# Row blocks of three, the last columns in halves and the last store in three pieces, in a windowed matrix product on one Trainium2 core

## The chip, the cores and the metric

The kernel runs on 1 core of one Trainium2 chip. The metric is the device time of one execution in microseconds (us). All timed runs compared here are of the fast state (two slow executions of the kernel before, 210.19 and 194.12 us, are left out); the five probe runs are single runs, whose state is unknown and whose time is not used.

## The reference

```python
B, S, D, W = 4, 4096, 4096, 64          # x is [B, S, D], w is [D, D], both fp32
for b in range(B):
    o = int(offsets[b])
    results.append(x[b, o:o+W] @ w)      # four windows of 64 rows, one matrix
return np.stack(results).astype(np.float32)
```

The 4 x 64 window rows are two groups `g` of 128. The matrix has 67 MB and is read once; that is most of the traffic of 75.5 MB.

## The kernel before

The matrix comes in by row blocks of 128 rows each ("row" in this text often means such a row of blocks, `ki` from 0 to 31). Up to row 21 whole rows are loaded, several in one DMA; from row 22 on (`k_tail`) the two column halves are loaded and finished one after the other, half 1 first. All these loads but that of row 0 are issued by GpSimd and are cast to fp16 on the way; row 0 comes by SP and ACT as fp32 and is cast by ACT.

```python
blocks = [(0, 1), (1, 1), (2, 4), (6, 4), (10, 4), (14, 4), (18, 2), (20, 2)]
k_tail = 22
...
order = [1, 0]
for ng in order:
    big = wc_pool.tile([P, R_MAX * N], fp16, name="wc", tag="wc")
    small = w1_pool.tile([P, N], fp16, name="w1", tag="w1")
    ki = k_tail
    while ki < n_k:
        n = 1 if ng == order[-1] and ki >= n_k - 2 else 2
        ...                                       # one DMA for n rows of this half
...
q = [nc.scalar, nc.sync]
for ng in order:
    ...
    for ki in kts:
        for g in range(G):
            for j in range(n_sub):                # 4 column tiles of 512
                ...
                mm(4 * g + j, g, ki, rhs, ki == kts[0], ki == kts[-1])
    for g in range(G):
        for j in range(n_sub):
            add_out(4 * g + j, g, ng * n_sub + j) # VectorE: acc += PSUM bank
    for g in range(G):
        (nc.gpsimd if ng == order[0] else q[g]).dma_start(
            out=out[2 * g : 2 * g + 2, :, ng * NG : (ng + 1) * NG],
            in_=acc[g][:, ng * NG : (ng + 1) * NG],
        )
```

## Time and profile before

| | before |
|---|---|
| median of 3 runs | 182.32 us (182.32 to 182.44) |
| profiled span | 180.37 us |
| HBM read and written | 71.30 + 4.19 MB, 419 GB/s |
| last stores issued (ACT, SP) | 172.83 and 175.21 us |

The way to read it is shown in the prediction below. In short: the DMA engines are full from start to end, TensorE waits for them in places, and the end is four stores of 1 MB, two of which fill the DMA engines while the other two are still being computed.

### The profile page before, as it was taken

The page shows a single profiled execution, that of the slowest core. Times are in us where ns is not written, and L with a number is a line of the kernel's source. Part 1 is how long each engine was busy: PE and PEld are TensorE (multiplying, and loading weights), DVE is VectorE, ACT ScalarE, POOL GpSimd, SP SyncE. Part 2 cuts the span into 40 slices and gives each one's busy share as a digit, 9 for nine tenths or more (in the row PEclk, how much of TensorE's full clock was granted, in tenths as well). Part 3 has the DMA queues.
Part 4 walks back from the last instruction along what each step waited for, and adds up shares of the span by engine and source line. Part 5 has one row for each costly group of instructions (what it writes and reads, how often), then busy time and mean ns, then how long its engine had stood idle before and what let it go on. Part 6 is the DMA issues. An engine that isn't in the chain of part 4 may idle for free.

```text
span 180.4 us, 1501 instructions
## 1 busy us (share of the span) xinstructions
PE 127.1 (70%) x576; PEld 57.8 (32%) x576; DVE 79.2 (44%) x120; ACT 14.4 (8%) x19; POOL 15.2 (8%) x30
## 2 busy tenths in 40 slices
PE   0000789504999399908996599999789998898900
PEld 0000774101344144303442244444234443343400
DVE  0000667400587277811886167899920007300280
ACT  2422546400000000000000000000000000000000
POOL 4600000000000100020002400041011001100000
PEclk9999999965799999996999879999999999999975
DMA  5999989999998899999999999999999999999986
GB/s 185 314 254 216 273 189 196 236 233 225 233 233 174 182 233 233 238 218 233 196 196 203 225 207 207 225 193 214 215 213 216 213 214 214 216 212 214 362 367 265
DMA packets 4936, 40.98 MB, mean 227 GB/s; under 512 B 450, under 2 KB 450, under 8 KB 3010
## 3 DMA queue, kind: packets, MB, share of 16 engines
q0 software_dynamic: 4352, 36.70, 94.2%
q1 hardware_dynamic: 288, 2.10, 3.1%
q10 hardware_dynamic: 290, 2.10, 2.8%
q8 instruction: 4, 0.07, 0.1%
q14 instruction: 2, 0.02, 0.0%
HBM read 71.30 MB, written 4.19 MB: 419 GB/s over the span
## 4 chain that ended last, share of the span: by engine, by line
DMA 57%; PE 29%; another core or an unknown queue 5%; issue 3%; DVE 1%; POOLq 1%; POOL 1%; DVEq 1%
DMA wc<-in_w_dram 57%; PE bank L143 29%; DVE acc L153 1%; POOLq L68 1%; DVEq L227 1%; POOL xrow L75 0%; POOL identity masks.py:197 0%; POOLq L75 0%; DVEq L153 0%; POOL w L64 0%; POOLq masks.py:199 0%; POOLq L216 0%
## 5 line engine op out<-in xcount | busy, mean ns | idle before, releaser
L143 PE MATMUL bank<-wc,xT 128*128 128x512 f16 x448 | 106.0, 394 | 25.1 <-DMA wc<-in_w_dram 22.4
L153 DVE TENSOR_TENSOR acc<-acc,bank 128x512 f32<-128x512 f32 x104 | 68.1, 685 | 72.8 <-PE bank L143 72.2
L143 PEld LDWEIGHTS <-xT 128*128 128x128 f16 x512 | 51.2, 101 | 93.6 <-DMA wc<-in_w_dram 23.6
L129 PE MATMUL bank<-identity,xrow 128*128 128x128 f16 x64 | 7.1, 312 | 19.6 <-DMA xrow<-in_x_dram 19.6
L138 DVE CAST xT<-bank 128x512 f16<-128x512 f32 x8 | 5.5, 692 | 21.5 <-PE bank L129 21.5
L143 PE MATMUL bank<-w,xT 128*128 128x512 f16 x64 | 14.6, 385 | 0.0
L129 PEld LDWEIGHTS <-xrow 128*128 128x128 f16 x64 | 6.7, 148 | 19.8 <-issue 19.8
L108 POOL DMA_DIRECT2D wc<-in_w_dram x8 | 5.6, 710 | 42.4 <-PE bank L143 36.0
L92 POOL DMA_DIRECT2D wc<-in_w_dram x6 | 3.2, 545 | 67.7 <-PE bank L143 67.7
L168 DVE COPY acc<-bank 128x512 f32<-128x512 f32 x8 | 5.5, 692 | 1.6 <-PE bank L143 1.4
L140 ACT CAST xT<-bank 128x512 f16<-128x512 f32 x8 | 4.7, 585 | 8.2 <-PE bank L129 8.2
L170 ACT COPY acc<-bank 128x512 f32<-128x512 f32 x8 | 4.7, 585 | 2.5 <-PE bank L143 2.5
L198 POOL DMA_DIRECT2D out_dram<-acc x2 | 1.1, 536 | 18.5 <-DVE acc L153 18.5
L108 POOL DMA_DIRECT2D w<-in_w_dram x3 | 1.8, 607 | 8.6 <-DMA wc<-in_w_dram 8.6
L61 ACT CAST w<-acc 128x2048 f16<-128x2048 f32 x1 | 1.9, 1897 | 4.7 <-DMA acc<-in_w_dram 4.7
L75 POOL DMA_DIRECT2D xrow<-in_x_dram x4 | 2.1, 524 | 2.1 <-issue 2.1
L60 ACT CAST w<-acc 128x2048 f16<-128x2048 f32 x1 | 1.9, 1897 | 2.9 <-DMA acc<-in_w_dram 2.9
L60 ACT ACT_TABLE_LOAD x1 | 1.3, 1283 | 1.8 <-PEq L216 1.8
L64 POOL DMA_DIRECT2D w<-in_w_dram x1 | 0.7, 667 | 0.8 <-POOLq L216 0.8
masks.py:199 POOL TENSOR_SCALAR_AFFINE_SELECT identity<-identity 128x128 f16<-128x128 f16 x1 | 0.3, 287 | 0.1
masks.py:197 POOL MEMSET identity<- 128x128 f16 x1 | 0.2, 223 | 0.0
L216 POOL MEMSET const-float32-0.0<- 128x1 f32 x1 | 0.1, 99 | 0.4 <-issue 0.4
(3 smaller groups left out, 0.3 us busy)
## 6 DMA issues: line engine op xcount, KB each, us to landing
wc<-in_w_dram POOLq DMA_DIRECT2D x4, 4096.0 KB, 48.3
wc<-in_w_dram POOLq DMA_DIRECT2D x8, 1024.0 KB, 36.5
wc<-in_w_dram POOLq DMA_DIRECT2D x2, 2048.0 KB, 38.8
w<-in_w_dram POOLq DMA_DIRECT2D x2, 1024.0 KB, 28.2
xrow<-in_x_dram POOLq DMA_DIRECT2D x4, 512.0 KB, 14.5
out_dram<-acc POOLq DMA_DIRECT2D x2, 1024.0 KB, 19.3
acc<-in_w_dram SPq DMA_DIRECT2D x1, 1024.0 KB, 5.1
acc<-in_w_dram ACTq DMA_DIRECT2D x1, 1024.0 KB, 11.2
```

The costliest lines, as they stand in the source:

```text
L60: nc.scalar.copy(out=w_one[0][:, :NG], in_=w0_32[:, :NG])
L61: nc.scalar.copy(out=w_one[0][:, NG:], in_=w0_32[:, NG:])
L75: nc.gpsimd.dma_start(out=x16[g][m * WIN : (m + 1) * WIN, :], in_=x[b][bass.ds(o, WIN), :],)
L92: nc.gpsimd.dma_start(out=t[:, base : base + r * N], in_=w[k0 * P : (k0 + r) * P, :].rearrange("(p r) n -> p (r n)", r=r),)
L108: nc.gpsimd.dma_start(out=t[:, c : c + n * NG].rearrange("p (t n) -> p t n", t=n), in_=w[ki * P : (ki + n) * P, ng * NG : (ng + 1) * NG].r ...
L129: nc.tensor.matmul(out=ps[t][:, i * P : (i + 1) * P], lhsT=x_cols(g, 4 * t + i), rhs=identity[:], start=True, stop=True,)
L138: nc.vector.tensor_copy(out=dst, in_=ps[t][:])
L140: nc.scalar.copy(out=dst, in_=ps[t][:])
L143: nc.tensor.matmul(out=ps[bank][:], lhsT=xT[g][:, kt * P : (kt + 1) * P], rhs=rhs, start=start, stop=stop,)
L153: nc.vector.tensor_add(out=dst, in0=dst, in1=ps[bank][:])
L168: nc.vector.tensor_copy(out=acc[g][:, c * NT : (c + 1) * NT], in_=ps[bank][:])
L170: nc.scalar.copy(out=acc[g][:, c * NT : (c + 1) * NT], in_=ps[bank][:])
```

## The change

The intent is a shorter end. Two rows of the matrix go from the column stage into blocks of three (fewer small packets). The last two rows of the last column half come in two quarters, so that half of the additions and stores can start earlier. ACT helps to empty the banks between the halves. The very last store is cut in pieces of 112, 8 and 8 rows, so that DMA engines 0 to 7 take nine rows and 8 to 15 take seven, on the premise that 8 to 15 are behind by then.

```diff
-    blocks = [(0, 1), (1, 1), (2, 4), (6, 4), (10, 4), (14, 4), (18, 2), (20, 2)]
-    k_tail = 22
+    blocks = [(0, 1), (1, 1), (2, 4), (6, 4), (10, 4), (14, 4), (18, 3), (21, 3)]
+    k_tail = 24
+    n_fine = 2
...
+    fine_steps = steps[: -(n_fine // 2)]
+    fine_steps.append((n_k - n_fine, n_fine, 0, NG // 2))
+    fine_steps += [(ki, 1, NG // 2, NG) for ki in range(n_k - n_fine, n_k)]
...
+    def store(eng, g, c0, c1, cuts=(0, P)):
+        for a, e in zip(cuts, cuts[1:]):
+            eng.dma_start(out=out_rows[g * P + a : g * P + e, c0:c1], in_=acc[g][a:e, c0:c1])
...
+    for g in range(G):
+        for j in range(0, n_sub, 2):
+            add_out(4 * g + j, g, ng * n_sub + j)
+            nc.scalar.copy(out=tmp[2 * g + j // 2][:], in_=ps[4 * g + j + 1][:])
...
+    for h in range(2):
+        js = range(h * n_sub // 2, (h + 1) * n_sub // 2)
...
+            c0 = ng * NG + h * NG // 2
+            store(q[g], g, c0, c0 + NG // 2, (0, 112, 120, 128) if h == g == 1 else (0, P))
```

More of the change, by code (lines that the diff above doesn't have):

```diff
@@ L41 @@
     wc_pool = ctx.enter_context(tc.tile_pool(name="wc", bufs=3))
-    w1_pool = ctx.enter_context(tc.tile_pool(name="w1", bufs=2))
+    w1_pool = ctx.enter_context(tc.tile_pool(name="w1", bufs=1))
     acc_pool = ctx.enter_context(tc.tile_pool(name="acc", bufs=1))
@@ L49 @@
     xT = [x_pool.tile([P, D], fp16, name=f"xT{g}") for g in range(G)]
-    w_one = [w1_pool.tile([P, N], fp16, name="w1", tag="w1") for i in range(2)]
+    w_one = [w1_pool.tile([P, N], fp16, name=f"w1_{i}") for i in range(2)]
+    tmp = [acc_pool.tile([P, NT], fp32, name=f"tmp{i}") for i in range(4)]
     acc = [acc_pool.tile([P, N], fp32, name=f"acc{g}") for g in range(G)]
@@ L84 @@
     }
-    free = 0
     for k0, r in blocks[2:]:
-        if free < r:
-            t = wc_pool.tile([P, R_MAX * N], fp16, name="wc", tag="wc")
-            free = R_MAX
-        base = (R_MAX - free) * N
-        free -= r
+        t = wc_pool.tile([P, R_MAX * N], fp16, name="wc", tag="wc")
         nc.gpsimd.dma_start(
-            out=t[:, base : base + r * N],
+            out=t[:, : r * N],
             in_=w[k0 * P : (k0 + r) * P, :].rearrange("(p r) n -> p (r n)", r=r),
@@ L96 @@
         for q in range(r):
-            src[k0 + q] = lambda a, e, t=t, c=base + q * N: t[:, c + a : c + e]
+            src[k0 + q] = lambda a, e, t=t, c=q * N: t[:, c + a : c + e]
     tail = {}
     order = [1, 0]
-    for ng in order:
-        big = wc_pool.tile([P, R_MAX * N], fp16, name="wc", tag="wc")
-        small = w1_pool.tile([P, N], fp16, name="w1", tag="w1")
-        ki = k_tail
-        while ki < n_k:
-            n = 1 if ng == order[-1] and ki >= n_k - 2 else 2
-            n_in = (ki - k_tail) * NG
-            t, c = (big, n_in) if n_in < R_MAX * N else (small, n_in - R_MAX * N)
+    steps = [(ki, 2, 0, NG) for ki in range(k_tail, n_k, 2)]
+    fine_steps = steps[: -(n_fine // 2)]
+    fine_steps.append((n_k - n_fine, n_fine, 0, NG // 2))
+    fine_steps += [(ki, 1, NG // 2, NG) for ki in range(n_k - n_fine, n_k)]
+    for ng, st in zip(order, (steps, fine_steps)):
+        t = wc_pool.tile([P, R_MAX * N], fp16, name="wc", tag="wc")
+        pos = 0
+        for ki, n, c0, c1 in st:
+            wd = c1 - c0
             nc.gpsimd.dma_start(
-                out=t[:, c : c + n * NG].rearrange("p (t n) -> p t n", t=n),
-                in_=w[ki * P : (ki + n) * P, ng * NG : (ng + 1) * NG].rearrange(
+                out=t[:, pos : pos + n * wd].rearrange("p (t n) -> p t n", t=n),
+                in_=w[ki * P : (ki + n) * P, ng * NG + c0 : ng * NG + c1].rearrange(
                     "(t p) n -> p t n", p=P
@@ L114 @@
             for q in range(n):
-                tail[(ng, ki + q)] = t[:, c + q * NG : c + (q + 1) * NG]
-            ki += n
+                for j in range(wd // NT):
+                    a = pos + q * wd + j * NT
+                    tail[(ki + q, (ng * NG + c0) // NT + j)] = t[:, a : a + NT]
+            pos += n * wd
     def x_cols(g, kt):
@@ L177, with tail_mm @@
     whole_rows(last_block, range(order[1] * n_sub, (order[1] + 1) * n_sub), False)
-    q = [nc.scalar, nc.sync]
-    for ng in order:
-        kts = list(range(k_tail, n_k))
-        if ng == order[0]:
-            kts = list(last_block) + kts
-        for ki in kts:
-            for g in range(G):
-                for j in range(n_sub):
-                    c = ng * n_sub + j
-                    rhs = (
-                        src[ki](c * NT, (c + 1) * NT)
-                        if ki < k_tail
-                        else tail[(ng, ki)][:, j * NT : (j + 1) * NT]
-                    )
-                    mm(4 * g + j, g, ki, rhs, ki == kts[0], ki == kts[-1])
+    def tail_mm(ki, g, ng, j, start, stop):
+        c = ng * n_sub + j
+        rhs = src[ki](c * NT, (c + 1) * NT) if ki < k_tail else tail[(ki, c)]
+        mm(4 * g + j, g, ki, rhs, start, stop)
@@ L194 @@
+    out_rows = out.rearrange("b m n -> (b m) n")
+    def store(eng, g, c0, c1, cuts=(0, P)):
+        for a, e in zip(cuts, cuts[1:]):
+            eng.dma_start(out=out_rows[g * P + a : g * P + e, c0:c1], in_=acc[g][a:e, c0:c1])
+    ng = order[0]
+    kts = list(last_block) + list(range(k_tail, n_k))
+    for ki in kts:
         for g in range(G):
             for j in range(n_sub):
-                add_out(4 * g + j, g, ng * n_sub + j)
-        for g in range(G):
-            (nc.gpsimd if ng == order[0] else q[g]).dma_start(
-                out=out[2 * g : 2 * g + 2, :, ng * NG : (ng + 1) * NG],
-                in_=acc[g][:, ng * NG : (ng + 1) * NG],
-            )
+                tail_mm(ki, g, ng, j, ki == kts[0], ki == kts[-1])
@@ new lines @@
+    for g in range(G):
+        for j in range(0, n_sub, 2):
+            add_out(4 * g + j, g, ng * n_sub + j)
+            nc.scalar.copy(out=tmp[2 * g + j // 2][:], in_=ps[4 * g + j + 1][:])
+    for g in range(G):
+        for j in range(1, n_sub, 2):
+            c = ng * n_sub + j
+            dst = acc[g][:, c * NT : (c + 1) * NT]
+            nc.vector.tensor_add(out=dst, in0=dst, in1=tmp[2 * g + j // 2][:])
+        store(nc.gpsimd, g, ng * NG, (ng + 1) * NG)
+    ng = order[1]
+    k_fine = n_k - n_fine
@@ new lines @@
+    for ki in range(k_tail, k_fine):
+        for g in range(G):
+            for j in range(n_sub):
+                tail_mm(ki, g, ng, j, ki == k_tail, False)
+    q = [nc.scalar, nc.sync]
+    for h in range(2):
+        js = range(h * n_sub // 2, (h + 1) * n_sub // 2)
+        for ki in range(k_fine, n_k):
+            for g in range(G):
+                for j in js:
+                    tail_mm(ki, g, ng, j, False, ki == n_k - 1)
+        for g in range(G):
+            for j in js:
+                add_out(4 * g + j, g, ng * n_sub + j)
+            c0 = ng * NG + h * NG // 2
+            store(q[g], g, c0, c0 + NG // 2, (0, 112, 120, 128) if h == g == 1 else (0, P))
```

## The prediction

> **What bounds the kernel now.** I read the page first: its slices, queues and HBM line, and then the chain that ended last.
>
> ```profile
> PE   0000789504999399908996599999789998898900
> DMA  5999989999998899999999999999999999999986
> q0 software_dynamic: 4352, 36.70, 94.2%
> HBM read 71.30 MB, written 4.19 MB: 419 GB/s over the span
> DMA 57%; PE 29%; another core or an unknown queue 5%; issue 3%; DVE 1%; POOLq 1%; POOL 1%; DVEq 1%
> ```
>
> The reader is to see that the DMA row has 9 nearly everywhere while PE has holes, and that 71.30 + 4.19 = 75.49 MB in 180.4 us is 419 GB/s. (The GB/s row of the page shows half of that during loads, because it counts the fp16 that is written.) The matrix is read once, so no bytes can be saved; only time in which a DMA engine does nothing, or moves its bytes badly, can.
>
> So I asked for the mean DMA share by stage. Columns: stretch, length, busy us of PE, PEld, DVE, ACT, POOL, granted clock, DMA share, GB/s.
>
> ```profile
> 62.40:82.00 19.60, 14.02 (x65) 6.22 (x66) 11.00 (x16) 0.00 (x0) 1.05 (x2) 1.00 1.00 215
> 125.80:164.70 38.90, 35.47 (x152) 14.69 (x151) 11.17 (x19) 0.00 (x0) 2.84 (x5) 1.00 1.06 214
> 168.00:172.00 4.00, 3.79 (x18) 1.52 (x16) 1.69 (x3) 0.00 (x0) 0.00 (x0) 1.00 1.02 411
> 172.00:173.00 1.00, 0.00 (x0) 0.00 (x0) 1.00 (x3) 0.00 (x0) 0.00 (x0) 1.00 0.87 369
> 173.00:174.00 1.00, 0.00 (x0) 0.00 (x0) 1.00 (x3) 0.00 (x0) 0.00 (x0) 0.99 0.53 221
> 175.00:178.00 3.00, 0.00 (x0) 0.00 (x0) 0.18 (x1) 0.00 (x0) 0.00 (x0) 0.50 0.99 412
> 178.00:179.00 1.00, 0.00 (x0) 0.00 (x0) 0.00 (x0) 0.00 (x0) 0.00 (x0) 0.50 0.67 279
> ```
>
> The engines are full in the block stage and in the column stage alike. The only hole before the end is at 172 to 174 us: 0.13 + 0.47 = 0.6 us of the mean engine. Then the timeline of the end:
>
> ```profile
> 164.72 3.61 PE L143 MATMUL bank<-wc,xT 128*128 128x512 f16 x16 [0.73 <-DMA wc<-in_w_dram]
> 168.17 3.62 PE L143 MATMUL bank<-w,xT 128*128 128x512 f16 x16
> 170.31 4.87 DVE L153 TENSOR_TENSOR acc<-acc,bank 128x512 f32<-128x512 f32 x8 [15.39 <-PE bank L143]
> 172.83 0.35 ACTq L198 DMA_DIRECT2D out_dram<-acc  x1
> 175.21 0.35 SPq L198 DMA_DIRECT2D out_dram<-acc  x1
> ```
>
> It looks like a tail worth cutting: the last rows arrive, 16 matmuls and 8 additions follow, and two 1 MB stores end the kernel. But the other two 1 MB stores, those of the first column half, stand in the GpSimd queue behind all loads, and feed the DMA engines in just this time. That is why the hole is 0.6 us and not the 8 us from the last load to the last store.
>
> The last view is the trace's packet records (start, length, size, queue of each packet). Each transfer ends with one small completion packet per engine. Of the 16 for the last GpSimd store eleven are at 173.0 to 173.6 us and five at 174.1 to 174.6. Of the last store (SP) twelve lie at 179.1 to 179.2, the others up to 179.49. So five engines run up to 1.5 us late. In the load stream an engine drops back, and stays back, six times: after a 16 KB instruction fetch (four, at 34.8, 76.0, 115.9 and 145.8 us) by about 1.1 us, after an 8 KB one (two, at 73.3 and 130.4) by about 0.5. The late engines have no hole at 172 to 174: the first HWDGE store's packets interleave with what they still owe. **The slowest engine is busy without a break from start to 179.49 us, and it sets the end.** The eleven others idle about 1 us and reach the same end within 0.4 us.
>
> **What the Trainium skill says.** (1) "Perfetto Trace Analysis", section Roofline, says that a single active core is bounded by its 16 DMA engines, about 435 GB/s. The trace agrees: 419 over the whole span, and in the block stage 1.05 MB x 2 per row in 4.85 us, 433. (2) "DMA: Bandwidth & Descriptors", section Why small descriptors are slow, gives each packet about 3 cycles on top of one for each 32 bytes. With the 850 MHz of its bandwidth section, an 8 KB source packet is 259 cycles, 304.7 ns; the packet records show one start each 304.6 ns per engine. So I use it for the other sizes, as estimates. (3) The same page, section Why a DMA increments its semaphore by 16, says that a transfer uses the largest k up to 16 that divides its outer dimension, on SP and ACT the lowest k engines: 112 rows would be 7 for each of 16 engines, 8 rows one for each of engines 0 to 7. No record here names an engine; that the late ones are among 8 to 15 is the premise of the change, which I can't check. (4) Its section Issuing engines are not separate DMA queues says that all queues share the 16 engines, which the interleaving of three queues at 174 us shows.
>
> **The change, part by part.**
>
> Blocks of 3 and 3 in place of 2 and 2, column stage from row 24 instead of 22. Per engine and row: 2-row packets 8 x 1208 / 2 = 4.833 us, 3-row 8 x 1811 / 3 = 4.828, column packets 16 x 304.7 = 4.875. Before, 4 rows x 4.833 + 2 x 4.875 = 29.08; after, 6 x 4.828 = 28.97. It saves 0.11 us.
>
> The last two rows in halves. That is one row's worth of bytes in 4 KB pieces, estimated at 131 cycles or 154.1 ns each: 32 x 154.1 = 4.93 in place of 4.875, costs 0.06.
>
> The stores of the last half in quarters: 4 KB pieces again, 32 x 154.1 against 16 x 304.7, costs 0.06. Some more completion packets: 0.03. These parts together come to +0.03 us on every engine, so nothing.
>
> The 112, 8, 8 rows: engines 8 to 15 have 7 pieces instead of 8, one piece of 154 ns less; 0 to 7 have one more. If the late engines are all in 8 to 15 the end comes 0.15 us sooner.
>
> The tail off the DMA. The loads still end at about 169.6. PE: the chunk of rows 28 and 29 lands at 164.7, 16 matmuls to 168.4, then 8 for the first quarter pair (170.2), 8 for the second (172.0, 0.226 us each from the rows above). Additions at 4.87 / 8 = 0.61: 169.7 to 172.1 and 172.1 to 174.5. Stores issued at about 171.0, 172.2, 173.4 and 174.6 to 175.7 (three of 0.35 on SP). Before, they went out at 172.83 and 175.21. From issue to the first packet the ACT store took 1.2 us (174.05), so the first now reaches the engines near 172.2, before the GpSimd stores end: the hole of 0.6 us on the mean engine closes. But it is on the fast engines only, which then end at about 178.2 instead of 179.1. The slow one has no hole to close.
>
> The freed banks: four ACT copies (0.585 each from the ACT group of this shape) beside four additions free the banks in about 2.4 instead of 4.9 us between the column halves. PE needs it, since the change gives it more to do late: the second 3-row block lands near 130.4 us, after that 24 + 88 + 32 = 144 matmuls x 0.226 = 32.5 us and about 1 us for the eviction bring it to 163.9, just ahead of the landing at 164.7. So it is spent in slack too.
>
> Sum for the slowest engine: 179.49 + 0.03 - 0.15 = 179.37. Last completion to the end of the span was 180.37 - 179.49 = 0.88: span 180.25. Measured time minus span was 182.32 - 180.37 = 1.95: **182.2 us**. As the instruction fetches may fall a little better on a program with the work cut differently, I say 182.1.
>
> **Rivals.**
>
> (A) The tail counts in full. If the final 1 MB store, 16 matmuls and 8 additions really were the path, halving the last store (1.2 us) and half of the additions (2.4 us) would give about 179 us. For it stands the chain of waits, which ends in the additions. Against it, DMA share 0.99 from 175 to 178 and the late engines without a gap. I give it 5%.
>
> (B) PE becomes the bound. It idles about 2.6 us before the second 3-row block (block done near 127.8). After the idle of 3.80 us at 101.35 the clock was granted at half and matmuls took 0.43 us; after 3.06 at 62.42 it wasn't. If it falls here, PE loses about 1.6 us and the last stores are issued at 175.5 to 176.5. The engines have work until about 177, so up to 0.5 us would be lost: 182.2 to 182.8.
>
> (C) The fetches hit other engines, or one engine twice: a second lag of 1.1 us on one engine would give 183.3. If a fetch moved behind the end of the work or the late engines were spread better, 181.5. If the late engine is among 0 to 7, the extra row costs 0.15: 182.5.
>
> (D) Small stores to HBM interleaved from three queues are less efficient than estimated. In the last stores of before, packets took 305 to 335 ns where two queues met: 5% on 1 MB is 0.15 us.
>
> **Range and chances.** The sum gives 182.1; C and D spread it by about 0.5 on either side, B adds a little above. The range is 181.5 to 182.7. A gain of 2% would need 178.7, which only (A) gives; a loss of 2% would need 186.0, for which PE would have to fall far behind: faster 0.03, same 0.95, slower 0.02.
>
> **What would show it right or wrong.** The share of DMA should be 1.0 at 172 to 174 us, the hole gone, and lower in the last microsecond, since the fast engines now end before the slow ones. Loads should end within 0.3 us of before. The last store should be issued near 175.5, while completion packets still end near 179.4. The waits should show PE waiting for the chunk of rows 28 and 29 by little or nothing, and about 2.6 us for the second 3-row block. It is wrong if the last completion comes before 178.7, which would mean that the late engines were not the bound, or if PE is late by more than 2 us, seen as stores issued after 177 and DMA shares under 0.9 before them.

## The result, and the profile after

| | before | changed |
|---|---|---|
| median of 6 runs | 182.32 us (182.16 to 182.44) | 183.17 us (182.98 to 183.60) |
| profiled span | 180.37 | 181.11 |

The ratio is 1.0048, 95% interval 1.0035 to 1.0061. (Ratios here are the mean time of one kernel's fast runs over that of the other's of the same rounds, so not quite the ratio of the medians quoted.) The change made the kernel 0.85 us slower, within the 2% but outside the predicted range.

First the page of the changed kernel: the DMA row of the slices, the large queue, the HBM line, the chain by engine.

```profile
DMA  5999979999999799999997999999999999999993
q0 software_dynamic: 4080, 36.70, 93.6%
HBM read 71.30 MB, written 4.19 MB: 417 GB/s over the span
DMA 63%; PE 26%; issue 3%; DVE 2%; POOL 1%; POOLq 1%; DVEq 0%
```

The bytes are the same and the engines are as full as before, but the last slice has 3 where it had 6: most engines are done earlier, and yet the end is later. The same stretches as in the prediction, for the changed kernel (columns as there):

```profile
125.80:164.70 38.90, 34.40 (x151) 14.96 (x150) 12.20 (x20) 2.05 (x4) 4.99 (x8) 0.96 1.04 209
168.00:172.00 4.00, 3.72 (x18) 1.47 (x15) 2.62 (x5) 0.00 (x0) 0.00 (x0) 1.00 1.03 413
172.00:173.00 1.00, 0.00 (x0) 0.00 (x0) 1.00 (x3) 0.00 (x0) 0.00 (x0) 1.00 0.96 406
173.00:174.00 1.00, 0.00 (x0) 0.00 (x0) 1.00 (x3) 0.00 (x0) 0.00 (x0) 1.00 1.01 418
175.00:178.00 3.00, 0.00 (x0) 0.00 (x0) 0.00 (x0) 0.00 (x0) 0.00 (x0) 0.65 0.99 397
178.00:179.00 1.00, 0.00 (x0) 0.00 (x0) 0.00 (x0) 0.00 (x0) 0.00 (x0) 0.50 0.33 131
```

The hole at 172 to 174 us is closed (0.96 and 1.01 where there were 0.87 and 0.53), and the last microsecond has 0.33 in place of 0.67. So the work of the mean engine did end sooner. The timeline of the end:

```profile
130.19 33.20 PE L144 MATMUL bank<-wc,xT 128*128 128x512 f16 x144 [3.14 <-DMA wc<-in_w_dram]
...
164.65 7.07 PE L144 MATMUL bank<-wc,xT 128*128 128x512 f16 x32 [1.27 <-DMA wc<-in_w_dram]
...
169.38 4.87 DVE L154 TENSOR_TENSOR acc<-acc,bank 128x512 f32<-128x512 f32 x8 [9.75 <-PE bank L144]
170.70 2.74 ACTq L189 DMA_DIRECT2D out_dram<-acc  x2
171.89 4.79 SPq L189 DMA_DIRECT2D out_dram<-acc  x4
```

TensorE, VectorE and the issue of the first stores are where the prediction had them, or a little sooner: 144 matmuls from 130.19 to 163.39, then a wait for rows 28 and 29, then additions from 169.38, stores from 170.70. What is new is on SP's queue. One line of the stores' own view for the changed kernel (count, then min/median/max in ns), and of the two kernels' last line (the waits at the end of the program) the SP part; the first pair is the changed kernel, the second the kernel before:

```profile
L189 SPq DMA_DIRECT2D out_dram<-acc x4: 346/594/1123, 171.9 to 175.6; - x4
```

```profile
L251 SPq EVENT_SEMAPHORE  x12: 17/28/28, 176.7 to 181.1; - x12
L251 SPq DRAIN  x3: 7/7/7, 180.3 to 180.6; - x3
```

```profile
L227 SPq EVENT_SEMAPHORE  x10: 17/28/28, 175.6 to 180.3; - x10
L227 SPq DRAIN  x3: 7/7/7, 179.5 to 179.8; - x3
```

Two of SP's four store issues took much longer than 0.35 us (by the records 0.83 and 1.12 us, the two of 8 rows). And SP reaches its first DRAIN at 180.3 instead of 179.5 us. The records of the trace show why. They give for each transfer when each engine's part has landed, and when each waiting instruction was let go:

```
                          last completion   last part    end of
                          packet            landed       span
before                    179.12            179.46       180.37   landing to end 0.90
changed                   179.33            179.76       181.11   landing to end 1.36

changed, SP after the last landing (us, semaphores waited for):
179.78 S107,S103   179.84 S108,S102   179.90 S109,S101   179.96 S115,S100
180.02 S116,S99    180.08 S117,S112   180.14 S118,S114   180.20 S119,S111
180.27 DRAIN
before: 179.48 S116,S102   179.55 DRAIN

changed, landings of the last three stores of SP (us):
112 rows  177.88 178.03 178.08 178.13 178.20 178.26 178.28 178.33 178.34 178.34 178.65 178.95 179.06 179.15 179.21 179.37
  8 rows  178.07 178.43 178.49 178.51 178.53 179.12 179.35 179.56
  8 rows  178.25 178.60 178.68 178.69 178.71 179.30 179.54 179.76
```

(A completion packet is the small packet with which an engine ends its part of a transfer; the landing is the semaphore update that follows.) So the 0.75 us of the span are 0.21 in the last completion packet, 0.09 between that packet and its landing, and 0.45 after the landing. The last is a list: at the end of the program SP checks the semaphores of all DMAs one after the other, 0.06 us each. In the kernel before the last store's semaphore is the last in the list, and all others have been checked while the store was under way. The changed kernel has nine DMAs on SP and ACT, three at the start and six stores, and the compiled program uses eight semaphores for them in turn:

```
3 L189 DMACopy out_0_dram<-acc1_86 112x1024 [waits DVE_49]
4 L189 DMACopy out_0_dram<-acc1_86 8x1024
5 L189 DMACopy out_0_dram<-acc1_86 8x1024 [waits DMAHW0_49]
```

The ninth takes the first one again (S107 here), which is near the front of the list, so seven more checks come after the last landing.

(The packet times in the prediction are 0.37 us too late against the span: I had taken the wrong zero of the records. With the right one the kernel before has its last completion at 179.12, not 179.49, and from an ACT issue to its first packet 0.85 us, not 1.2. Differences are not touched by this.)

### The profile page after: what moved, and what is told of

It is laid out like the page before. It is cut to its first block, busy times and chain, and to the rows that moved or that the text cites. A ratio compares the mean times of both kernels' runs of the same rounds, so it can differ in the third digit from the quotient of the medians.

```text
span 181.1 us, 1508 instructions
## 1 busy us (share of the span) xinstructions
PE 126.2 (70%) x576; PEld 57.0 (31%) x576; DVE 80.0 (44%) x120; ACT 16.2 (9%) x23; POOL 14.5 (8%) x29
## 4 chain that ended last, share of the span: by engine, by line
DMA 63%; PE 26%; issue 3%; DVE 2%; POOL 1%; POOLq 1%; DVEq 0%
DMA wc<-in_w_dram 63%; PE bank L144 26%; DVE acc L154 2%; POOL wc L108 1%; POOLq L70 1%; POOL xrow L77 0%; DVEq L251 0%; POOL identity masks.py:197 0%; POOLq L77 0%; POOL w L66 0%; POOLq masks.py:199 0%; DVEq L154 0%; POOLq L240 0%
## 5 line engine op out<-in xcount | busy, mean ns | idle before, releaser
L144 PE MATMUL bank<-wc,xT 128*128 128x512 f16 x480 | 113.8, 402 | 25.8 <-DMA wc<-in_w_dram 25.7
L154 DVE TENSOR_TENSOR acc<-acc,bank 128x512 f32<-128x512 f32 x100 | 67.0, 686 | 72.4 <-PE bank L144 71.6
L144 PEld LDWEIGHTS <-xT 128*128 128x128 f16 x512 | 51.9, 102 | 94.3 <-DMA wc<-in_w_dram 26.9
L130 PE MATMUL bank<-identity,xrow 128*128 128x128 f16 x64 | 5.5, 266 | 19.8 <-DMA xrow<-in_x_dram 19.8
L200 ACT COPY tmp<-bank 128x512 f32<-128x512 f32 x4 | 2.1, 600 | 122.1 <-PE bank L144 122.1
L130 PEld LDWEIGHTS <-xrow 128*128 128x128 f16 x64 | 5.1, 127 | 20.0 <-issue 20.0
L89 POOL DMA_DIRECT2D wc<-in_w_dram x6 | 3.2, 542 | 89.2 <-PE bank L144 89.2
L108 POOL DMA_DIRECT2D wc<-in_w_dram x10 | 6.7, 682 | 35.0 <-PE bank L144 25.3
L144 PE MATMUL bank<-w,xT 128*128 128x512 f16 x32 | 7.1, 379 | 0.0
L205 DVE TENSOR_TENSOR acc<-acc,tmp 128x512 f32<-128x512 f32 x4 | 2.5, 682 | 0.0
L66 POOL DMA_DIRECT2D w<-in_w_dram x1 | 0.7, 660 | 0.8 <-POOLq L240 0.8
```

The source lines that it names most:

```text
L89: nc.gpsimd.dma_start(out=t[:, : r * N], in_=w[k0 * P : (k0 + r) * P, :].rearrange("(p r) n -> p (r n)", r=r),)
L108: nc.gpsimd.dma_start(out=t[:, pos : pos + n * wd].rearrange("p (t n) -> p t n", t=n), in_=w[ki * P : (ki + n) * P, ng * NG + c0 : ng * NG ...
L130: nc.tensor.matmul(out=ps[t][:, i * P : (i + 1) * P], lhsT=x_cols(g, 4 * t + i), rhs=identity[:], start=True, stop=True,)
L144: nc.tensor.matmul(out=ps[bank][:], lhsT=xT[g][:, kt * P : (kt + 1) * P], rhs=rhs, start=start, stop=stop,)
L154: nc.vector.tensor_add(out=dst, in0=dst, in1=ps[bank][:])
L205: nc.vector.tensor_add(out=dst, in0=dst, in1=tmp[2 * g + j // 2][:])
```

## The experiments

Theory T: the loss is the wait list (0.43 us), plus an extra row on late engines that are in the half given more work. Rivals: the halves or the blocks cost it; the splitting of the store costs it by itself; the late engines are not made by instruction fetches at all.

| run | edit in the changed kernel, where not said otherwise | median, us | before in the same rounds | ratio, 95% interval |
|---|---|---|---|---|
| plain_last | last store in one piece | 182.26 | 182.37 | 0.9992 (0.9979 to 1.0006) |
| two_pieces | 112 + 16 rows | 182.61 | 182.37 | 1.0014 (1.0000 to 1.0027) |
| after_last_wait | seven tiny loads more at the start | 182.73 | 182.37 | 1.0023 (1.0009 to 1.0037) |
| before_early_wait | kernel before, four tiny loads more | 182.78 | 182.37 | 1.0023 (1.0009 to 1.0036) |
| two_halves | 64 + 64 rows | 182.27 | 182.27 | 1.0003 (0.9989 to 1.0018) |
| before_low_rows | kernel before, 2 x 8 rows more for engines 0 to 7 | 182.45 | 182.27 | 1.0011 (0.9996 to 1.0026) |
| before_no_fetch | kernel before, 54 matmuls | 181.38 | 182.27 | 0.9953 (0.9939 to 0.9967) |
| plain_no_fetch | plain_last, 54 matmuls | 181.45 | 182.27 | 0.9960 (0.9947 to 0.9974) |
| no_halves | last columns whole | 182.12 | 182.31 | 0.9997 (0.9983 to 1.0011) |
| contiguous_pieces | 64 + 32 + 16 + 16 rows | 182.63 | 182.34 | 1.0020 (1.0008 to 1.0033) |
| strided_pieces | the same, every 2nd, 4th, 8th, 8th row | 182.70 | 182.34 | 1.0020 (1.0007 to 1.0033) |
| pieces_96_32 | 96 + 32 rows | 182.66 | 182.41 | 1.0018 (1.0004 to 1.0033) |
| pieces_16_112 | 16 + 112 rows | 182.32 | 182.41 | 0.9997 (0.9984 to 1.0010) |

All gave correct results but the two "no_fetch" kernels, which are wrong on purpose (the expectation below says 55 matmuls; the code and both traces have 54). On some of the chips the kernel before itself falls into two groups (181.96 to 182.06 and 182.27 to 182.59 in the rounds of two_halves), so differences under 0.2 us are not read from medians alone.

### The last store in one piece: plain_last

```diff
-            store(q[g], g, c0, c0 + NG // 2, (0, 112, 120, 128) if h == g == 1 else (0, P))
+            store(q[g], g, c0, c0 + NG // 2, (0, P))
```

> The changed kernel with its last store in one piece of 128 rows. Theory T: of the 0.75 us by which the profiled span grew (180.37 to 181.11), 0.43 us is the list of semaphore waits that SP works off at the end (the last 8-row store has a semaphore that stands early in the list), about 0.3 us is the extra row on engines 0 to 7, three of which are among the five late ones. Both go: about 182.2 us, within 0.3 of before, last completion packet within 0.1 us of before's. Rival R1 (the halves of the last columns and their 4 KB pieces cost it, in the loads or stores): it stays near 183.0. Rival R2 (the change's own premise, late engines are 8 to 15, the split helps and only the wait list hurts): 182.2 to 182.4 too, but last completion later than in the changed kernel by 0.15 us.

It was 182.26 us, level with before: the whole 0.9 us is in the three pieces, and the blocks, the halves and the ACT copies together are worth nothing that these runs can tell from zero (the interval is about 0.25 us wide on either side). The hole is closed here too, and the late engines still end at the same place. Windows of plain_last:

```profile
173.00:174.00 1.00, 0.00 (x0) 0.00 (x0) 1.00 (x3) 0.00 (x0) 0.00 (x0) 1.00 0.98 406
...
178.00:179.00 1.00, 0.00 (x0) 0.00 (x0) 0.00 (x0) 0.00 (x0) 0.00 (x0) 0.50 0.27 111
```

At 173 to 174 us the share is 0.98 in place of 0.53, in the last microsecond 0.27 in place of 0.67; the first engines end at 177.60 instead of 178.70 us, and the last one at 179.29 instead of 179.12. The expected "within 0.1 of before's last completion" was missed by 0.07 in this one profile.

### The wait list, in both directions: after_last_wait and before_early_wait

```diff
+    for i in range(7):          # 4 in the kernel before; never read
+        nc.sync.dma_start(out=spare[:, i * B : (i + 1) * B], in_=offsets[None, :])
```

> The changed kernel with seven more loads of 32 bytes at the start (never read), so that the last 8-row store gets the last of the eight semaphores instead of the first again. Nothing of the stores is changed. Theory T: the time from the landing of the last store to the end of the span falls from 1.36 us to about 0.9, the time by about 0.4 us, to 182.7 to 182.8; the last completion packet stays about 0.2 us later than in before. Rival R3 (late issue of the small stores): no change, 183.1.

> The kernel before with four more loads of 32 bytes at the start (never read), so that its last store, the ninth DMA of SP and ACT, gets the first of the eight semaphores again. Its stores, loads and engines are as before. Theory T: landing unchanged within 0.1 us, from landing to the end 1.3 us instead of 0.90, time about 182.7. Rivals: no change, 182.3.

With sixteen DMAs in all the last store gets the last semaphore of the eight; with nine in the kernel before, its last store gets the first again. No byte that matters and no engine's share is moved. The SP lines of the waits at the end, first after_last_wait, then before_early_wait:

```profile
L254 SPq DRAIN  x3: 7/7/7, 179.9 to 180.2; - x3
```

```profile
L230 SPq DRAIN  x3: 7/7/7, 180.0 to 180.3; - x3
```

By the records, after_last_wait has its last landing at 179.81 (changed kernel: 179.76) and the end 0.93 us later (1.36); before_early_wait has it at 179.47 (before: 179.46) and the end 1.35 us later (0.90). The times went from 183.17 to 182.73 (in other rounds, in which the kernel before differed by 0.05) and from 182.37 to 182.78. Both directions give 0.4 us. The mechanism is shown.

### What is left: pieces of the last store

After the wait list, 182.73 - 182.26 = 0.47 us are left between after_last_wait and plain_last. The next runs take the extra row away, or cut the store in other places; each edit is one tuple, for instance

```diff
-            store(q[g], g, c0, c0 + NG // 2, (0, 112, 120, 128) if h == g == 1 else (0, P))
+            store(q[g], g, c0, c0 + NG // 2, (0, 112, 128) if h == g == 1 else (0, P))
```

> The last store as 112 and 16 rows: every engine has 7 + 1 rows, as many as with one piece, but there is one more DMA than in plain_last, issued late. Theory T: no engine has an extra row and the semaphores do not wrap round (8 DMAs on SP and ACT in all), so as plain_last within 0.15 us, about 182.2 to 182.4. Rival R3 (splitting itself, late issue and one more completion, is what costs): half way between plain_last and the changed kernel or more, 182.6 to 183.0.

Here every engine has eight rows again, and the wait list is right (0.93 us from landing to end), but the time is 182.61: 0.35 above plain_last in the same rounds. What the extra row costs can't be had from 182.73 - 182.61 = 0.12, which is within the scatter of the two; the records give it at the end of this part. Theory T was too simple, and rival R3 has a point. The records show two oddities: SP took 1.83 us to issue the second piece, and four packets (three of ACT's store, which was under way at 176 us, one of SP's) took 0.41 to 0.69 us where 0.159 is usual. So I asked whether any second piece does this.

> The last store as 64 and 64 rows (4 + 4 rows for every engine, no extra row, eight DMAs on SP and ACT, no semaphore used twice). In two_pieces (112 + 16) the second store took SP 1.83 us to issue in place of 0.35, and four store packets took 0.4 to 0.7 us in place of 0.16 while it was being issued; the median was 0.35 us above plain_last. Theory T2: it is the further DMA, queued right behind another on the same queue, that does this, whatever its rows: again 0.3 us above plain_last, about 182.6, with long packets near 176 us. Rival: it is the small number of rows per engine (1): then as plain_last, 182.3, and no packet over 0.34 us.

No: 182.27, no packet over 0.22 us. It is not one more DMA as such. Is it the pieces with one row per engine, which all come from a few neighbouring partitions?

> The last store in pieces of 64, 32, 16 and 16 neighbouring rows: 4 + 2 + 1 + 1 rows for each engine, no extra row, ten DMAs on SP and ACT (so 0.4 us for the wait list, as in the changed kernel). Theory P: 16 engines that read one row each of 16 neighbouring partitions meet at the few SBUF ports of these partitions; by the port formula of the Trainium skill, page SBUF — State Buffer, section Door 1: The DMA port swizzle, rows 96 to 111 and 112 to 127 lie on four ports each, so a packet can take up to four times 0.159 us: packets of 0.4 to 0.65 us, 183.0 to 183.2. Rival (short transfers as such are slow, or their issue): the same here.

> The same four sizes, but each piece takes every 2nd, 4th, 8th and 8th row, so that the 16 rows of a piece lie on eight ports. Nothing else differs from contiguous_pieces. Theory P: no packet over 0.34 us, and 0.2 to 0.4 us sooner than contiguous_pieces: 182.7 to 182.8. Rival: packets of 0.4 us and more, and the time of contiguous_pieces.

```diff
+                for a0, step in ((0, 2), (1, 4), (3, 8), (7, 8)):
+                    q[g].dma_start(
+                        out=out_rows[g * P + a0 : (g + 1) * P : step, c0 : c0 + NG // 2],
+                        in_=acc[g][a0:P:step, c0 : c0 + NG // 2],
+                    )
```

The packets did what theory P said: ten of the contiguous kernel's 4 KB packets took over 0.2 us, up to 0.42, against three of the strided one's, up to 0.23. But the times are alike, 182.63 and 182.70, and both have the wait list against them (1.29 us from landing to end, 0.38 more than plain_last). Less that, both are level with plain_last. So one row per engine at the end costs nothing that can be seen, and long packets need not reach the end. The last two runs cut once more in two.

> The last store as 96 and 32 rows (6 + 2 rows for every engine, eight DMAs on SP and ACT, no semaphore used twice). Theory Q (a piece whose rows per engine are no multiple of four sets the engines on each other's SBUF ports and costs the 0.3 us): 182.6, long packets as in two_pieces. Theory S (the single row per engine behind a large piece costs it): as plain_last, 182.2 to 182.3.

> The last store as 16 and then 112 rows (1 + 7 rows for every engine). Theory Q: 182.6 as two_pieces, since the 112 rows are in it. Theory S: 182.2 to 182.3, since the single rows are not at the end. If both runs are level with plain_last, the 0.35 us of two_pieces stays unexplained.

96 + 32 rows took 182.66, as 112 + 16; 16 + 112 took 182.32. Neither theory fits: 112 rows cost nothing when they come second, and the cost is there without single rows. What the runs allow to say is this. Where SP's first piece is one of 96 or 112 rows with a smaller one behind it (two_pieces, pieces_96_32, after_last_wait, the changed kernel), packets of ACT's own store, running beside it at 176 to 178 us, took up to 0.6 to 0.84 us, and the median is longer (two_pieces 0.35 us above plain_last, pieces_96_32 0.34 above pieces_16_112, each pair in the same rounds); where the first piece is of 16, 64 or 128 rows, no packet of ACT's store was over 0.2 us and the time, less the wait list, is that of plain_last. A slow issue is not enough to cost time: pieces_16_112 took 1.21 us to issue its second piece and lost nothing. The cause of the long packets stays open.

The records do tell what reached the end in the profiled executions. The view is the time from the moment at which the latest engine completes its part of the last GpSimd store (174.21 us before, 174.16 in the changed kernel) to the last completion packet of the last store:

```
before, before_early_wait, before_low_rows, before_no_fetch, no_halves    4.91 in each
plain_last 4.99; two_halves, pieces_16_112, pieces_96_32 5.00; contiguous_pieces, strided_pieces 5.01
changed kernel, after_last_wait 5.16
two_pieces 5.18
```

So the halves cost 0.08 to 0.10 us at the end, and the extra row with its further completion packets 0.17 (5.16 against 4.99). In two_pieces the 0.18 arises in ACT's store, where the latest engine is done 3.93 us after the GpSimd store in place of 3.75: a long packet was on that engine. In the profiles of the changed kernel, after_last_wait and pieces_96_32 the long packets were on other engines (3.74 to 3.75 for the latest) and cost nothing. Whether they are on the latest engine in most executions, which would give the longer medians, is not shown, as one execution of each kernel is profiled.

### Which engines are late: before_low_rows and the probes

```diff
+    for i in range(2):          # kernel before; SP; never read
+        nc.sync.dma_start(out=spare[:, i * 1024 : (i + 1) * 1024], in_=w[0:8, i * 1024 : (i + 1) * 1024])
```

> The kernel before with two more loads at the start, each of 8 rows of 4 KB (never read): two more pieces of about 0.155 us on engines 0 to 7, none on 8 to 15, far from the end. Theory T: the latest engine of all is one of 0 to 7 (in the changed kernel the latest of the 8 landings of the 8-row store lies, less two pieces, at the latest of the 112-row store): the end comes 0.3 us later, 182.65. The premise of the change (latest engines are among 8 to 15, ahead by more than two pieces): no change, 182.35.

182.45 against 182.27, with an interval that holds both zero and 0.4 us: inconclusive by its median. Three runs took 182.16 to 182.26 and three 182.64 to 182.93. In the profiled one, of the upper group, the last landing was at 180.14 instead of 179.46. By its records a fetch at 115.1 us came to an engine that was already 1.07 us behind the first one; at the last GpSimd store it was 2.16 us behind (before: 1.56), and the 4.91 us after it were the same. This is the second lag on one engine of rival C; for the other long executions of this kernel it is not shown.

The probes read the engines directly, without any cost of stores in pieces.

```diff
+    for i, (eng, n) in enumerate([(nc.scalar, 4), (nc.scalar, 2), (nc.scalar, 1), (nc.sync, 8)]):
+        eng.dma_start(out=probe[:n, 8 * i : 8 * i + 8], in_=w[:n, :8])
```

> plain_last with four loads of 32 bytes a row right behind the last stores: 4, 2 and 1 rows on ACT, 8 rows on SP. Their completions come when the engine has worked off its part of the store ahead in the same queue, so they name which of engines 0, 1, 2 to 3, 4 to 7 and 8 to 15 are late. The time itself is of no interest. Premise of the change: all 8 completions of the SP probe lie among the early ones (within 0.6 us). Theory T: two or three of the 8 are late by 0.5 to 1.5 us.

> The same kernel as probe_1, once more: is the set of late engines the same in each run? before_low_rows took 182.16 to 182.26 in three of six runs and 182.64 to 182.93 in the others, as if the latest engine were sometimes in the one half and sometimes in the other. Theory T: the number of late engines in 0 to 7 differs from run to run.

> The same kernel a third time, as probe_2. Theory T: another number or other ones of the 8 are late. Rival: the same ones in all three runs, so that a fixed shift of rows could be aimed at them.

> As probe_1, with probes of 8, 7 and 6 rows on ACT and 7 rows on SP. Where the latest engine is 7, the 8-row probe on ACT has a completion near the end of the ACT store's last one and the 7- and 6-row probes have none; where it is one of 4 to 6, the 7-row probes have it too. Theory: I lean to 7, 60 to 40, as the Trainium skill (DMA: Bandwidth & Descriptors, section Latency and other measured facts) calls engines 7 and 15 usually slower.

> As probe_7a, once more: the same engine again if it is a fixed one, another if it changes from run to run.

```
us           SP's last store, landings 10 to 16 of 16                 SP probe of 8 rows (about 0.2 later than the store)
probe_1      178.65 178.73 178.89 178.96 179.23 179.25 179.69         178.38 178.57 178.81 178.82 178.92 179.07 179.15 179.89
probe_2      178.52 178.59 179.23 179.32 179.40 179.42 179.58         178.58 178.65 178.66 178.77 178.80 179.57 179.62 179.78
probe_3      178.66 178.66 178.98 179.01 179.33 179.40 179.61         178.74 178.75 178.84 178.84 178.91 179.15 179.21 179.80

             ACT's last store, landings 12 to 16 of 16                ACT probe of 8 rows
probe_7a     177.73 177.97 178.01 178.07 178.33                       177.24 177.36 177.38 177.46 177.48 177.93 178.15 178.54
probe_7b     177.80 177.88 177.95 177.96 178.09                       177.16 177.21 177.36 177.38 177.43 177.99 178.08 178.15
```

Of the 16 parts of the store five stand apart as late in all runs but probe_1, where the gap is blurred. Three of these five are among the eight of the probe, so among engines 0 to 7 by the rule under (3) of the prediction (no record names an engine), and two are in 8 to 15. The very latest is among 0 to 7 in probe_1, 2, 3 and 7a (its probe lies 0.19 to 0.21 after the store's latest) and among 8 to 15 in 7b (the latest probe, 178.15, less 0.2 is 177.95, not 178.09). In 7a the 7-row probe of SP has the latest engine (180.00 against 179.80 of the store) and the 6-row probe hasn't: it was engine 6. My lean to engine 7 was wrong, and it is not always the same engine. The premise of the change, late engines in 8 to 15, holds in none of the five runs. The landings of the 8-row stores above say the same of the changed kernel: three late ones out of eight, and the latest of these, less the two pieces of about 0.2 us, lies at the latest of the 112-row store. Its five late engines complete the 112 rows at 178.59, 178.71, 178.78, 178.85 and 178.99 us. The 8-row stores add 0.16 us each on the first, third and fifth, to 178.91, 179.10 and 179.32. The other two are done at once, 4.84 us after the GpSimd store, 0.15 sooner than with a whole store. The saving was there, on engines that were not the latest.

### What makes them late: before_no_fetch and plain_no_fetch

```diff
-                for i, kt in enumerate(kts):
-                    mm(bank, g, kt, src[kt](c * NT, (c + 1) * NT), i == 0, i == len(kts) - 1)
+                if not first and (g or c != cols[0]):
+                    continue
+                kt = kts[-1]
+                mm(bank, g, kt, src[kt](c * NT, (c + 1) * NT), True, True)
```

and in the same way one transposition in four and only the last row in the column stage.

> Wrong on purpose: the kernel before with all its loads and stores, but only 55 matmuls and as many weight loads, so that the TensorE program is about 110 instructions and needs no 16 KB instruction fetch. The last 8 matmuls stand where they stood. Theory T: no engine falls back by 1.1 us, the completions of the last GpSimd store lie within 0.8 us (before: 1.56), the last completion of all is at 178.7 to 178.9 instead of 179.12 because the hole before the last stores stays: 182.0. Rival (the five engines are slow by nature, or fall back for another reason): spread 1.5 us, 182.35.

> Wrong on purpose: plain_last cut down in the same way. Theory T: with no late engine the closed hole is worth its 0.6 to 1.0 us at last: last completion at about 178.1, 181.3 us, about 0.7 us under before_no_fetch, where with the fetches plain_last and before are alike within 0.1. Rival (late engines not made by the fetches): equal to plain_last and to before_no_fetch, 182.3.

Loads and stores are all there. The queues of before_no_fetch (packets, MB, share of 16 engines), which list no instruction queue any more:

```profile
q0 software_dynamic: 4352, 36.70, 94.5%
q1 hardware_dynamic: 288, 2.10, 3.2%
q10 hardware_dynamic: 290, 2.10, 2.8%
```

The 16 completions of the last GpSimd store now lie at 172.66 to 173.38 us, 0.72 apart, where in the kernel before they lie at 172.66 to 174.22. The fast engines are where they were; the late ones are gone. The last completion of all is at 178.29 instead of 179.12 and the time 0.9 us less. These kernels also lack nine matmuls in ten, but the records of the kernel before show the same without an edit. Distances of the 16 completions from the first, in us, for three GpSimd transfers (named by the time of the first):

```
 22.09  0.00 0.00 0.06 0.08 0.11 0.19 0.23 0.25 0.30 0.40 0.40 0.44 0.47 0.48 0.51 0.60
 41.41  0.00 0.00 0.06 0.08 0.12 0.19 0.25 0.30 0.40 0.40 0.44 0.47 0.48 0.51 0.60 1.36
172.65  0.00 0.08 0.11 0.19 0.25 0.29 0.39 0.47 0.47 0.50 0.59 1.09 1.11 1.35 1.48 1.56
```

The one 16 KB fetch between the first two (34.4 us) moved one engine from 0.23 to 1.36. The distances change after the six fetches and otherwise stay within 0.01 us: one engine moves by 1.09 to 1.13 us after each of 16 KB and by 0.53 after each of 8 KB. In before_no_fetch they stay within 0.01 us from 12 to 173 us. So the instruction fetches make the late engines. Half of the test failed: I had expected before_no_fetch to keep its hole and plain_no_fetch to gain 0.7 us by closing it, but they are alike (181.38, 181.45). The short program also issues its last stores 0.8 us sooner (172.03 in place of 172.83), which closes the hole by itself:

```profile
172.00:173.00 1.00, 0.18 (x1) 0.00 (x0) 1.00 (x2) 0.00 (x0) 0.00 (x0) 1.00 1.03 434
173.00:174.00 1.00, 0.00 (x0) 0.00 (x0) 1.00 (x3) 0.00 (x0) 0.00 (x0) 1.00 0.99 418
```

What the closed hole would be worth without late engines is left open by these two.

### The halves alone: no_halves

```diff
-    fine_steps.append((n_k - n_fine, n_fine, 0, NG // 2))
-    fine_steps += [(ki, 1, NG // 2, NG) for ki in range(n_k - n_fine, n_k)]
+    fine_steps = steps[:-1] + [(ki, 1, 0, NG) for ki in range(n_k - n_fine, n_k)]
...                              # and the last half stored whole, one DMA for each g
```

> The changed kernel with its blocks of 3 and 3 and its ACT copies, but the last columns whole: last rows in whole halves of the matrix as before, and the two last stores whole with 8 KB rows. The prediction gave the blocks 0.11 us to the good, the halves 0.12 us to the bad, and the hole that the halves close nothing, since only the early engines have it. Theory T: 182.2, within 0.2 of plain_last and of before. Rival (the halves help by what they close): 182.7 or more.

182.12 against 182.31 of before, ratio 0.9997: the blocks and copies without the halves are level with before, and with plain_last. The halves help nothing and harm nothing. plain_last, two_halves, no_halves and pieces_16_112 all have medians about 0.5% under the changed kernel's (in other rounds); none of the correct versions tried beats the kernel before clearly.

## Why the prediction was wrong

- **The bound: right.** The slowest DMA engine set the end: in the five kernels with whole last stores the end of the last transfer came 4.91 us after the latest engine's part of the last GpSimd store, whether that was at 173.37 us (before_no_fetch) or at 174.87 (before_low_rows). Loads ended where they had (last completion of the last load 169.27 in the changed kernel, 169.31 before), TensorE and VectorE were early enough. TensorE's wait for the second block was 3.14 us, not 2.6, and its clock did drop afterwards (mean 0.96 in 125.8 to 164.7 us), as rival B feared, but it still had 1.27 us in hand at rows 28 and 29.
- **Blocks, halves and 4 KB pieces, +0.03 us: right** as far as the runs resolve it: plain_last 0.9992, no_halves 0.9997. Its part for the last stores, 0.06 + 0.03, measured 0.08 (4.99 against 4.91).
- **The hole closes and gains nothing: right**, by the windows of plain_last. Rival A is out.
- **"To 0 to 7 one more, to 8 to 15 one piece of 154 ns less: 0.15 us sooner": wrong, in sign.** I had called it the premise of the change that I could not check, and then put it in the sum at its full size. Three of five late engines are in 0 to 7, mostly with the latest. In the changed kernel's own trace the late engines in 8 to 15 did save 0.15 us, but the latest is in 0 to 7 and paid 0.17 (5.16 against 4.99). Rival C named this, with nearly the right size (0.15), as the less likely case.
- **"Three of 0.35 on SP": wrong.** The issues of 8 rows took 0.83 and 1.12 us. By themselves they were in time. But with a first piece of 112 rows and a smaller one behind it the median rose by 0.35 us (two_pieces against plain_last), a term that the sum did not have. Its cause is open.
- **"Last completion to the end of the span was 0.88": wrong as a constant.** That stretch holds a list of waits whose length depends on where the last transfer's semaphore stands in it. From landing to end it was 1.36 instead of 0.90, which cost 0.44 us, half of the whole loss (183.17 against 182.73).
- **The sum.** In the two profiles: -0.05 (the latest engine at the last GpSimd store, which differs between executions) + 0.08 (halves) + 0.17 (extra row) + 0.09 (from packet to landing) + 0.45 (wait list) = 0.74 of the 0.75 us by which the span grew. The prediction had 0.03 - 0.15 in place of it. The profiled execution is the shortest of the changed kernel's six (182.98 us, median 183.17), so about 0.2 us of a usual one is in no profile; the long packets may be it, which is not shown.
- **Late engines come from the instruction fetches: right**, shown by the kernel before's own records and by the two kernels without fetches.

## What to carry to other kernels

When DMA engines are the bound, ask for the latest engine, not the mean: a hole that only the early engines have is worth nothing. Before cutting a last store into more DMAs, count the DMAs of that kind in the whole program: a semaphore used a second time can stand early in the list of waits at the end, and each check behind it costs 0.06 us. A shift of work between engines needs a reading of which engines are late, in several executions, since here it changed; a few loads of 32 bytes a row behind the last store give it.

## What the Trainium skill lacked or had wrong

- "Runtime: NRT & Kernel Launch", section Instruction fetch mechanics, calls the cost of crossing a 16 KiB boundary "mostly hidden". TensorE did not stand still at the fetches of 72.9, 115.5 and 145.4 us (no gap over 0.1 us), but one of the same DMA engines fell back by about 1.1 us at each fetch of 16 KB. In this DMA-bound kernel the program without fetches, which also issued its last stores 0.8 us sooner, had its last completion 0.83 us sooner.
- No page says that the program's end checks the DMA semaphores one by one and that their order matters: 0.06 us each, 0.44 us for the changed kernel.
- "DMA: Bandwidth & Descriptors", section Latency and other measured facts, calls engines 7 and 15 usually slower. In probe_7a the latest engine was 6, in probe_7b one of 8 to 15, in probe_1, 2 and 3 one of 0 to 7 but not of 0 to 3. Without instruction fetches no engine is slower than another: in before_no_fetch their distances stay within 0.01 us from 12 to 173 us.
- No page says that a store issued from SP right behind another can take longer to issue: as the second one 64 rows took 0.63 us, 8 rows 0.83, 112 rows 1.21 and 16 rows 1.83; as the first, 0.35 us for 16 or 112 rows (0.53 for 64).
- "SBUF — State Buffer", section Door 1: The DMA port swizzle, fits the packets (up to 0.42 us from neighbouring rows, up to 0.23 us from every eighth row), but the time did not follow it (182.63 and 182.70 us).
